# Neighbourhood attention in a two-layer backbone: two heads of a couple as one unit instead of one head after the other

## The chip, the cores and the metric

One Trainium2 chip, one of its cores. The metric is device time in microseconds (us) of one launch; lower is better. The kernel is written in Bass with the Tile framework: the program is Python that emits instructions, and a scheduler fixes, when the program is built, in which order each engine (TensorE = PE, VectorE = DVE, ScalarE = ACT, GpSimd = POOL, SyncE = SP) gets them. On the chip each engine takes its own list strictly in that order, and semaphores make it wait for the others.

## What is computed

Two trunk layers of a diffusion backbone over 384 tokens (128 context, 256 latent) of width 1024. In each layer the tokens go through an input projection, four mixing branches (retention, an S5 state-space scan, gated linear attention, neighbourhood attention), gates, a merge, an output projection and an MLP. The change is in the neighbourhood attention. It has 4 heads of 64 channels. For a block of 128 queries and a head, cut to what matters:

```python
s = q @ k.T * 0.125                 # context block: 128 keys; latent block: 256 latent keys + 128 cached context keys
s[:, :256] += bias                  # latent blocks only: a table with the window of neighbours
p = softmax(s)                      # over all keys of the row
o = p @ v
```

There are three blocks of queries (one context, two latent) and four heads, so 12 such pieces a layer.

## The kernel before, in words

Nearly all of TensorE's time is weights: a tile of 128 x 1024 float32 weights is loaded (`next_w`, L167), split into a rounded high part and a low part (ACT cast L143, DVE subtraction L155), and multiplied in three terms (L208, L209, L210), 24 matmuls a tile. Everything else is put between these: after each weight tile `step` (L193) advances every running background job, a Python generator, by its rate. In `mixers` (L1436) the jobs are the S5 scan (`s5_scan` L957, 31 dependent steps on POOL), `na_mix` (L1358, the neighbourhood attention, at `NA_RATE`), `gla_mix` and `ret_mix`. What the generators emit is then placed by the scheduler, so the order of an engine follows neither the text nor the generators alone.

`na_mix` takes one head at a time: for a pair `pr` of heads, a block `i` of queries and a head `par` of the pair it does

- scores on PE (L1377): q and k of head `par` lie in partitions 64*par to 64*par+63, so the matmul uses half of the array's rows and fills one PSUM bank (tag `my`, which `yps` gives out and of which there are only two); float32, so it goes through the array in two passes;
- for latent blocks a DMA of the bias table (L1380, SP queue), the sum on DVE (L1381) and a copy on ACT (L1382); for the context block a copy (L1384);
- softmax: maximum on DVE (L1386), exponential with its sum on ACT (L1387), reciprocal and scaling on DVE (L1388, L1389);
- then `yield`, and transposes on PE (L1393) into a second `my` bank, a copy on ACT (L1394), the values (L1397, half of the array's columns, one to three matmuls of two passes each), and a copy of 64 partitions into `q` (L1399).

Its scratch is the row buffer `rB`, three slots of 1024 columns in rotation. The whole job is 12 units of two yields, at rate 2: 12 weight tiles.

After the projection `mixers` waits for the S5 scan and the attention to be emitted (`finish`), then `s5_spread` (L985) takes `rB` over: two memsets on DVE (L990) and 12 copies on ACT (L994, L995, L996) of the scan's result. L994 and L996 read all time slots, so they need the last step of the scan; the S5 output matmuls (L1016, L1020) and the gates (`gates` L1405, their activation L1411 writes `rC`, which holds the scan's result) come behind. Beside them run the last parts of the gated linear attention (L1118, L1200 to L1232) and of the retention (L1287 to L1324).

Of the kernel before, what the change touches and what calls it, by code (L numbers as in the profile page):

```python
# [15 lines left out]
AF = mybir.ActivationFunctionType  # L16
ALU = mybir.AluOpType
ADD, SUB, MUL = ALU.add, ALU.subtract, ALU.mult
# [24 lines left out]
RAW4 = 4  # L43
LAG0 = 2
ADA_MIX, ADA_MLP, S5_MLP = (5, 4), (2, 1), (4, 1)
NA_RATE = 2
FOUR = ([((0, 1, 2), (k,)) for k in range(3)] + [((3,), range(3))] + [(range(4), (k,)) for k in range(3, 6)]
        + [((b,), (6, 7)) for b in range(4)])

# [5 lines left out]
class Kernel:  # L55
# [1302 lines left out]
    def na_mix(self, l):  # L1358
        nc = self.nc
        V, A = nc.vector, nc.scalar  # L1360
        q, k, v = self.nq, self.nk, self.nv
        cv = self.ft[:, 2694:2950]
        nc.gpsimd.dma_start(cv, self.d["na_v"][l])
        rb = self.row("rB", shape=(128, 3072))
        unit = 0
        for pr in range(2):
            for i in range(3):
                for par in range(2):

                    h = 2 * pr + par  # L1370
                    r = slice(64 * par, 64 * par + 64)
                    n = 384 if i else 128
                    o = 1024 * (unit % 3)
                    unit += 1
                    s, pT, bias = rb[:, o:o + n], rb[:, o + 384:o + 384 + n], rb[:, o + 768:o + 1024]
                    ps = self.yps()
                    nc.tensor.matmul(ps[:, 0:n], q[r, pr, 128 * i:128 * (i + 1)], k[r, pr, 128:512] if i else k[r, pr, 0:128],  # L1377
                                     start=True, stop=True)
                    if i:
                        nc.sync.dma_start(bias, self.d["na_bias"][l, pr, :, par, i - 1])  # L1380
                        V.tensor_tensor(s[:, 0:256], ps[:, 0:256], bias, op=ADD)  # L1381
                        A.copy(s[:, 256:384], ps[:, 256:384])  # L1382
                    else:
                        A.copy(s, ps[:, 0:n])  # L1384
                    mx, sm, rs = self.few(1), self.few(1), self.few(1)
                    V.tensor_reduce(mx, s, axis=mybir.AxisListType.X, op=ALU.max, negate=True)  # L1386
                    A.activation(s, s, AF.Exp, bias=mx, accum_out=sm)  # L1387
                    V.reciprocal(rs, sm)  # L1388
                    V.tensor_scalar(s, s, rs, None, op0=MUL)  # L1389
                    yield  # L1390
                    pt = self.yps()
                    for j in range(n // 128):
                        nc.tensor.transpose(pt[:, j * 128:(j + 1) * 128], s[:, j * 128:(j + 1) * 128], self.ident)  # L1393
                    A.copy(pT, pt[:, 0:n])  # L1394
                    vs = [v[:, 1], v[:, 2], cv] if i else [v[:, 0]]
                    for j, lv in enumerate(vs):
                        nc.tensor.matmul(pt[r, 384:512], lv[:, h * 64:(h + 1) * 64], pT[:, j * 128:(j + 1) * 128],  # L1397
                                         start=j == 0, stop=j == len(vs) - 1)
                    A.copy(q[r, pr, 128 * i:128 * (i + 1)], pt[r, 384:512])  # L1399
                    yield  # L1400
        self.out[3] = q


# [32 lines left out]
    def mixers(self, l, hs, hook, first):  # L1436
# [5 lines left out]
        self.na_in(l, hs, first)  # L1442
        na = self.start(self.na_mix(l), NA_RATE)
        self.gla_in(l, hs)
# [359 lines left out]
```

## Time and profile before

| | |
|---|---|
| runs, us | 1440.46, 1439.47, 1440.29 (median 1440.29) |
| the profiled execution, us | 1436.91 |
| its span from first to last instruction, us | 1435.0 |
| granted TensorE clock, mean | 0.993 |
| PE busy | 1383.7 us, 96% |
| DVE, ACT, POOL busy | 65%, 46%, 24% |

PE is the bound, so an instruction on another engine costs time only where PE comes to wait for it. A row of the timeline gives the start, the duration, the engine, the line, the operation and, in brackets, the idle time ahead of it with what ended it. Matmuls overlap in the array: what one costs is the distance from its start to the next start, not its duration.

### The profile page before, as it was taken

How to read it: one execution, taken by the hardware profiler on the slowest of the kernel's cores; microseconds unless marked ns; L12 is line 12 of the kernel's file. 1: busy time of each engine (PE TensorE's matmuls, PEld its weight loads, DVE VectorE, ACT ScalarE, POOL GpSimd, SP SyncE). 2: the span in 40 equal slices, each digit the busy share in tenths (PEclk: the TensorE clock that was granted, in tenths of full speed). 3: DMA queues.
4: the chain of work that ended last, by engine and by line, in shares of the span. 5: the costliest groups of instructions: out<-in, count | busy, mean ns of one | idle time of the engine just before them, and what ended most of it. 6: DMA issues, size and time to landing. Idle time of an engine off the chain costs nothing. (4 is left out here: it accounts for less than half of the span.)

```text
span 1435.0 us, 22364 instructions
## 1 busy us (share of the span) xinstructions
PE 1383.7 (96%) x8492; PEld 1230.5 (86%) x8492; DVE 936.5 (65%) x1480; ACT 664.1 (46%) x1235; POOL 350.5 (24%) x654
## 2 busy tenths in 40 slices
PE   6979999999999999999999999999999999999998
PEld 5857867899998888888988888698999789999896
DVE  4598972699875868777363388448995658333334
ACT  3446563433336544443464555643433465444433
POOL 5964691001121123320011592000011200000000
PEclk9999999999999999999999999999999999999999
DMA  9446433477553656666446433146764536333442
GB/s 383 150 132 188 148 103 82 158 231 238 191 177 131 196 181 202 197 216 205 151 144 198 144 102 105 56 140 211 250 218 133 205 104 220 132 125 125 136 150 82
DMA packets 93628, 238.17 MB, mean 166 GB/s; under 512 B 17968, under 2 KB 39504, under 8 KB 93520
## 3 DMA queue, kind: packets, MB, share of 16 engines
q1 hardware_dynamic: 90656, 227.75, 49.0%
q0 software_dynamic: 2864, 8.98, 1.9%
q8 instruction: 67, 1.10, 0.3%
q14 instruction: 41, 0.34, 0.1%
HBM read 221.72 MB, written 14.97 MB: 165 GB/s over the span
## 5 line engine op out<-in xcount | busy, mean ns | idle before, releaser
L155 DVE TENSOR_TENSOR wl<-wf,wh 128x1024 fp32r<-128x1024 f32 (+1 forms) x254 | 320.6, 1265 | 269.8 <-ACT wh L143 269.2
L143 ACT CAST wh<-wf 128x1024 fp32r<-128x1024 f32 (+1 forms) x254 | 264.4, 1045 | 433.5 <-PE mx L209 175.2
L208 PE MATMUL mm<-hh,wh 128*128 128x384 f32 (+1 forms) x712 | 243.8, 342 | 1.4 <-ACT fb L879 1.4
L210 PE MATMUL mm<-hh,wl 128*128 128x384 f32 (+1 forms) x712 | 242.6, 342 | 1.1 <-DVE wl L155 1.1
L209 PE MATMUL mm<-hl,wh 128*128 128x384 f32 (+1 forms) x712 | 242.3, 340 | 0.0
L208 PE MATMUL mx<-hh,wh 128*128 128x384 f32 x448 | 151.1, 337 | 0.0
L210 PE MATMUL mx<-hh,wl 128*128 128x384 f32 x448 | 150.5, 336 | 0.0
L209 PE MATMUL mx<-hl,wh 128*128 128x384 f32 x448 | 150.4, 336 | 0.0
L210 PEld LDWEIGHTS mm<-hh,wl 128*128 128x128 f32 (+1 forms) x712 | 133.0, 187 | 7.3 <-issue 4.0
L208 PEld LDWEIGHTS mm<-hh,wh 128*128 128x128 f32 (+1 forms) x712 | 133.0, 187 | 6.7 <-issue 2.8
L209 PEld LDWEIGHTS mm<-hl,wh 128*128 128x128 f32 (+1 forms) x712 | 133.1, 187 | 6.2 <-issue 4.2
L604 DVE SCALAR_TENSOR_TENSOR mid<-r,fa 128x1024 f32<-128x1024 f32 x80 | 102.6, 1283 | 30.9 <-DMA r<-w_ada 20.6
L604 DVE SCALAR_TENSOR_TENSOR mid<-r,fb 128x1024 f32<-128x1024 f32 x80 | 100.1, 1251 | 0.2
L209 PE MATMUL mm<-wl,rA 128*128 128x512 f32 x216 | 85.7, 397 | 1.5 <-DVE wl L155 1.5
L208 PEld LDWEIGHTS mx<-hh,wh 128*128 128x128 f32 x448 | 84.2, 188 | 2.8 <-issue 1.0
L209 PEld LDWEIGHTS mx<-hl,wh 128*128 128x128 f32 x448 | 84.2, 188 | 1.8
L210 PEld LDWEIGHTS mx<-hh,wl 128*128 128x128 f32 x448 | 84.2, 188 | 0.2
L208 PE MATMUL mm<-wh,rA 128*128 128x512 f32 x216 | 79.5, 397 | 0.7 <-ACT rA L121 0.7
L210 PE MATMUL mm<-wh,rB 128*128 128x512 f32 x180 | 70.2, 392 | 0.0
L1431 POOL TENSOR_TENSOR c<-c,c 128x384 f32<-128x384 f32 x16 | 16.6, 1038 | 189.8 <-DVE c L1429 115.6
L706 POOL TENSOR_TENSOR few<-few,negh 128x1 f32<-128x1 f32 x24 | 13.3, 555 | 200.7 <-DVE few L705 194.6
L121 ACT CAST rA<-c 128x384 fp32r<-128x384 f32 x80 | 41.1, 514 | 40.4 <-DVE c L1433 38.6
(539 smaller groups left out, 2940.9 us busy)
## 6 DMA issues: line engine op xcount, KB each, us to landing
wf<-w_mlp SPq DMA_DIRECT2D x128, 512.0 KB, 3.5
r<-w_ada SPq DMA_DIRECT2D x82, 512.0 KB, 4.2
wf<-w_merge SPq DMA_DIRECT2D x64, 512.0 KB, 4.0
wf<-w_in SPq DMA_DIRECT2D x43, 512.0 KB, 4.0
wf<-w_branch SPq DMA_DIRECT2D x16, 512.0 KB, 4.1
wf<-w_out SPq DMA_DIRECT2D x16, 512.0 KB, 3.5
s_vt<-mid SPq DMA_DIRECT2D x16, 256.0 KB, 3.1
mid<-s_vt SPq DMA_DIRECT2D x8, 512.0 KB, 5.0
```

The costliest lines, as they stand in the source:

```text
L121: self.nc.scalar.copy(hi, src)
L143: self.nc.scalar.copy(wh[:, :cols], raw)
L155: self.nc.vector.tensor_tensor(wl[:, :cols], raw, wh[:, :cols].bitcast(F32), op=SUB)
L208: mm(out, lh, rh, start=start, stop=False)
L209: mm(out, lh, rl, start=False, stop=False)
L210: mm(out, ll, rh, start=False, stop=stop)
L604: nc.vector.scalar_tensor_tensor(self.mid([128, D]), w, 0.5, self.cb[g], op0=MUL, op1=MUL, accum_out=mod[:, n, g:g + 1])
L706: self.nc.gpsimd.tensor_tensor(r, v, self.negh[:, 0:1], op=ALU.pow)
L1431: nc.gpsimd.tensor_tensor(us[0], us[0], us[1], op=ADD)
```

## The change

The head leaves the loop and becomes a loop inside the unit: both scores go into two banks, then the softmax of the one and of the other, then the transposes of both into two banks, then the values of both into two halves of the partitions of one bank, alternating between the heads, and one copy of 128 partitions into `q`. The bias tables move into four slots behind the two heads' scratch, which no longer rotates: every unit uses the same two slots. There are six units of two yields a layer, and `NA_RATE` is 1, so the job still takes 12 weight tiles.

```diff
--- before.py
+++ after.py
@@ -43,7 +43,7 @@
 RAW4 = 4
 LAG0 = 2
 ADA_MIX, ADA_MLP, S5_MLP = (5, 4), (2, 1), (4, 1)
-NA_RATE = 2
+NA_RATE = 1
 FOUR = ([((0, 1, 2), (k,)) for k in range(3)] + [((3,), range(3))] + [(range(4), (k,)) for k in range(3, 6)]
         + [((b,), (6, 7)) for b in range(4)])
 
@@ -1362,42 +1362,51 @@
         cv = self.ft[:, 2694:2950]
         nc.gpsimd.dma_start(cv, self.d["na_v"][l])
         rb = self.row("rB", shape=(128, 3072))
-        unit = 0
-        for pr in range(2):
-            for i in range(3):
+        for u in range(6):
+
+
+            pr, i = divmod(u, 3)
+            n = 384 if i else 128
+            qs = slice(128 * i, 128 * (i + 1))
+            w = [rb[:, o:o + 1024] for o in (0, 1024)]
+            s = [t[:, 0:n] for t in w]
+            ps = [self.yps() for _ in w]
+            for par in range(2):
+                r = slice(64 * par, 64 * par + 64)
+                nc.tensor.matmul(ps[par][:, 0:n], q[r, pr, qs], k[r, pr, 128:512] if i else k[r, pr, 0:128],
+                                 start=True, stop=True)
+            for par in range(2):
+                if i:
+                    bias = rb[:, 2048 + 256 * (2 * (u % 2) + par):][:, 0:256]
+                    nc.sync.dma_start(bias, self.d["na_bias"][l, pr, :, par, i - 1])
+                    V.tensor_tensor(s[par][:, 0:256], ps[par][:, 0:256], bias, op=ADD)
+                    A.copy(s[par][:, 256:384], ps[par][:, 256:384])
+                else:
+                    A.copy(s[par], ps[par][:, 0:n])
+            mx, sm, rs = self.few(2), self.few(2), self.few(2)
+            for par in range(2):
+                c = slice(par, par + 1)
+                V.tensor_reduce(mx[:, c], s[par], axis=mybir.AxisListType.X, op=ALU.max, negate=True)
+                A.activation(s[par], s[par], AF.Exp, bias=mx[:, c], accum_out=sm[:, c])
+            for par in range(2):
+                c = slice(par, par + 1)
+                V.reciprocal(rs[:, c], sm[:, c])
+                V.tensor_scalar(s[par], s[par], rs[:, c], None, op0=MUL)
+            yield
+            pt = [self.yps() for _ in w]
+            pT = [t[:, 384:384 + n] for t in w]
+            for par in range(2):
+                for j in range(n // 128):
+                    nc.tensor.transpose(pt[par][:, j * 128:(j + 1) * 128], s[par][:, j * 128:(j + 1) * 128], self.ident)
+                A.copy(pT[par], pt[par][:, 0:n])
+            vs = [v[:, 1], v[:, 2], cv] if i else [v[:, 0]]
+            for j, lv in enumerate(vs):
                 for par in range(2):
-
                     h = 2 * pr + par
-                    r = slice(64 * par, 64 * par + 64)
-                    n = 384 if i else 128
-                    o = 1024 * (unit % 3)
-                    unit += 1
-                    s, pT, bias = rb[:, o:o + n], rb[:, o + 384:o + 384 + n], rb[:, o + 768:o + 1024]
-                    ps = self.yps()
-                    nc.tensor.matmul(ps[:, 0:n], q[r, pr, 128 * i:128 * (i + 1)], k[r, pr, 128:512] if i else k[r, pr, 0:128],
-                                     start=True, stop=True)
-                    if i:
-                        nc.sync.dma_start(bias, self.d["na_bias"][l, pr, :, par, i - 1])
-                        V.tensor_tensor(s[:, 0:256], ps[:, 0:256], bias, op=ADD)
-                        A.copy(s[:, 256:384], ps[:, 256:384])
-                    else:
-                        A.copy(s, ps[:, 0:n])
-                    mx, sm, rs = self.few(1), self.few(1), self.few(1)
-                    V.tensor_reduce(mx, s, axis=mybir.AxisListType.X, op=ALU.max, negate=True)
-                    A.activation(s, s, AF.Exp, bias=mx, accum_out=sm)
-                    V.reciprocal(rs, sm)
-                    V.tensor_scalar(s, s, rs, None, op0=MUL)
-                    yield
-                    pt = self.yps()
-                    for j in range(n // 128):
-                        nc.tensor.transpose(pt[:, j * 128:(j + 1) * 128], s[:, j * 128:(j + 1) * 128], self.ident)
-                    A.copy(pT, pt[:, 0:n])
-                    vs = [v[:, 1], v[:, 2], cv] if i else [v[:, 0]]
-                    for j, lv in enumerate(vs):
-                        nc.tensor.matmul(pt[r, 384:512], lv[:, h * 64:(h + 1) * 64], pT[:, j * 128:(j + 1) * 128],
-                                         start=j == 0, stop=j == len(vs) - 1)
-                    A.copy(q[r, pr, 128 * i:128 * (i + 1)], pt[r, 384:512])
-                    yield
+                    nc.tensor.matmul(pt[0][64 * par:64 * par + 64, 384:512], lv[:, h * 64:(h + 1) * 64],
+                                     pT[par][:, j * 128:(j + 1) * 128], start=j == 0, stop=j == len(vs) - 1)
+            A.copy(q[:, pr, qs], pt[0][:, 384:512])
+            yield
         self.out[3] = q
 
 
```

What the scheduler makes of it, at three places. On PE around the third and fourth piece of layer 0, before (L1377 scores, L1393 transposes, L1397 values, `mm` a weight tile, L532 and L566 the S5 set-up):

```order
L1393 MATMUL my_1226<-ident_76,rB_1051 128x128 x2
L1377 MATMUL my_1321<-fa_781,fb_782 128x384
L208 MATMUL mm_1281<-wh_1173,hh_394 128x256
...
L209 MATMUL mm_1479<-hl_395,wh_1282 128x384
L1397 MATMUL my_1226<-rB_1051,fb_782 64x128 [waits Activation_49]
L1397 MATMUL my_1226<-rB_1051,fb_782 64x128
L1397 MATMUL my_1226<-rB_1051,rE_780 64x128 [waits DMASW2_49]
L210 MATMUL mm_1479<-hh_394,wl_1283 128x384
```

and now (L1406 values, L1376 scores):

```order
L1406 MATMUL my_1317<-rB_1051,fb_782 64x128 [waits Activation_49]
L208 MATMUL mm_1471<-hh_394,wh_1278 128x384
...
L1406 MATMUL my_1317<-rB_1051,fb_782 64x128 [waits Activation_49]
L1406 MATMUL my_1317<-rB_1051,fb_782 64x128 x2
L1406 MATMUL my_1317<-rB_1051,rE_780 64x128 [waits DMASW2_49]
L1406 MATMUL my_1317<-rB_1051,rE_780 64x128
L1376 MATMUL my_1411<-fa_781,fb_782 128x384 [waits PE_49]
```

The first head's first value matmul now stands by itself, the other five alternate between the heads, and the first score of the next unit stands right behind them; that unit's second score follows 27 rows later (it needs a bank).

On PE at the end of the input projection of layer 0, before (`mm_2887` is the last projected weight tile; the attention still has two pieces to go):

```order
L210 MATMUL mm_2887<-hh_394,wl_2596 128x384
L1393 MATMUL my_2230<-ident_76,rB_1051 128x128 [waits DVE_49,Activation_49]
L1393 MATMUL my_2230<-ident_76,rB_1051 128x128 x2
L1200 MATMUL mx_2624<-rX_1003,g_490_2605 128x512 [waits PE_49,Activation_49]
L1200 MATMUL mx_2631<-rX_1003,g_490_2605 128x512 [waits PE_49]
L1287 MATMUL mx_2644<-ident_76,r_497_2637 128x128 [waits PE_49]
L1377 MATMUL my_2306<-fa_781,fb_782 128x384 [waits Activation_49]
L1397 MATMUL my_2230<-rB_1051,fb_782 64x128 [waits Activation_49]
```

and now (`mm_2863` is that weight tile):

```order
L210 MATMUL mm_2863<-hh_394,wl_2572 128x384
L1406 MATMUL my_2286<-rB_1051,fb_782 64x128 [waits Activation_49]
L1406 MATMUL my_2286<-rB_1051,fb_782 64x128 x2
L1406 MATMUL my_2286<-rB_1051,rE_780 64x128 x2
...
L1298 MATMUL my_2757<-r_479_2613,rs_2610 128x256
L1200 MATMUL mx_2600<-rX_1003,g_472_2581 128x512 [waits PE_49,Activation_49]
L1200 MATMUL mx_2607<-rX_1003,g_472_2581 128x512 [waits PE_49]
L1287 MATMUL mx_2620<-ident_76,r_479_2613 128x128 [waits PE_49]
L1020 MATMUL my_2646<-rB_2554,mid_2647 128x96 [waits DMAHW1_49,DVE_49,Activation_49]
```

The attention ends with the weight tile, and the first S5 output matmul that reads the spread scan (L1020) has moved up: it stands ahead of the retention's and the linear attention's L1291, L1206, L1210 and L1222, which stood ahead of it.

On ACT at the same place, before (L1201 and L1289 evict L1200's and L1287's banks, L1212 and L1208 the linear attention's):

```order
L1201 COPY rA_1004<-mx_2624 128x512 [waits PE_49]
L1201 COPY rA_1004<-mx_2631 128x512 [waits PE_49]
L1289 COPY c_499_2646<-mx_2644 128x128 [waits PE_49]
...
L1212 COPY g_520_2747<-mx_2745 128x256 [waits DMASW0_49,PE_49]
L1399 COPY fb_782<-my_2318 64x128 [waits PE_49]
L994 COPY rB_2578<-rC_1658 64x384 [waits DVE_49,DMAHW4_49,Activation_49,Pool_49]
L995 COPY rB_2578<-rC_1658 64x8x16
```

and now (L1420 is the gates' activation):

```order
L1198 COPY rX_1003<-g_473_2582 32x128 x4
L994 COPY rB_2554<-rC_1642 64x384 [waits Pool_49]
L996 COPY rB_2554<-rC_1642 64x8x32
...
L996 COPY rB_2554<-rC_1642 64x8x32
L1201 COPY rA_1004<-mx_2600 128x512 [waits PE_49]
L1201 COPY rA_1004<-mx_2607 128x512 [waits PE_49]
L1289 COPY c_481_2622<-mx_2620 128x128 [waits PE_49]
L1420 ACTIVATE rC_2569<-mm_2570,bmh_742 128x384 [waits Activation_49]
```

The copies of the scan, which wait for POOL, stood behind L1201, L1289, L1294, L1208, L1212 and L1308; now they stand ahead of all of these, which are in the same queue.

## Rows read from the trace of the kernel before

**Rows 1.** The page, busy time of each engine.

```profile
PE 1383.7 (96%) x8492; PEld 1230.5 (86%) x8492; DVE 936.5 (65%) x1480; ACT 664.1 (46%) x1235; POOL 350.5 (24%) x654
```

**Rows 2.** Timeline of PE, a piece's transposes and the next piece's scores.

```profile
109.24 0.49 PE L1393 MATMUL my<-ident,rB 128*128 128x128 f32 x3
109.66 0.91 PE L1377 MATMUL my<-fa,fb 64*128 64x384 f32 x2
110.50 0.38 PE L208 MATMUL mm<-wh,hh 128*128 128x256 f32 x1
```

**Rows 3.** Timeline of PE, a piece's values between matmuls of a weight tile.

```profile
113.72 0.34 PE L208 MATMUL mm<-hh,wh 128*128 128x384 f32 x1
113.89 0.34 PE L209 MATMUL mm<-hl,wh 128*128 128x384 f32 x1
114.16 0.65 PE L1397 MATMUL my<-rB,fb 128*64 128x128 f32 x4
...
114.96 0.44 PE L210 MATMUL mm<-hh,wl 128*128 128x384 f32 x1
115.24 0.34 PE L208 MATMUL mm<-hh,wh 128*128 128x384 f32 x1
```

**Rows 4.** Timeline of PE in layer 1, scores with values right behind them.

```profile
905.19 0.91 PE L1377 MATMUL my<-fa,fb 64*128 64x384 f32 x2
906.03 0.65 PE L1397 MATMUL my<-rB,fb 128*64 128x128 f32 x4
...
906.83 0.49 PE L1291 MATMUL mx<-rD,c 128*128 128x128 f32 x2
```

**Rows 5.** Timeline of PE in layer 1, two heads' matmuls in the two column halves.

```profile
913.31 0.27 PE L1231 MATMUL mx<-rA,rE 128*64 128x128 f32 x1
913.37 0.27 PE L1229 MATMUL mx<-rA,rE 128*64 128x128 f32 x1
913.42 0.27 PE L1231 MATMUL mx<-rA,rE 128*64 128x128 f32 x1
```

**Rows 6.** Timeline of POOL, the scan of layer 0: first step, sixteenth, last instruction.

```profile
153.13 0.36 POOL L976 TENSOR_TENSOR sm<-sm,rC 128x64 f32<-128x64 f32 x1 [26.97 <-ACT rC L953]
...
195.93 0.61 POOL L979 TENSOR_TENSOR rC<-sm,sm 128x32 f32<-128x32 f32 x1
...
219.41 0.26 POOL L981 TENSOR_TENSOR rC<-sm,sm 128x32 f32<-128x32 f32 x1
```

**Rows 7.** Timeline of PE, layer 0, between the last projected and the next weight tile.

```profile
202.57 0.45 PE L210 MATMUL mm<-hh,wl 128*128 128x384 f32 x1
...
223.92 1.13 PE L1298 MATMUL my<-r,rs 128*128 128x256 f32 x4
...
226.08 0.35 PE L1020 MATMUL my<-rB,mid 128*128 128x96 f32 x1 [0.45 <-ACT rB L994]
...
235.27 0.63 PE L208 MATMUL mm<-hh,wh 128*128 128x384 f32 x1
```

**Rows 8.** Timeline of ACT, the first copy of the spread in layer 0.

```profile
222.66 0.51 ACT L994 COPY rB<-rC 64x384 f32<-64x384 f32 x1
```

**Rows 9.** Windows: us, busy us of PE, PEld, DVE, ACT, POOL, granted clock, DMA.

```profile
75.00:82.00 7.00, 0.19 (x2) 0.00 (x0) 7.00 (x8) 0.11 (x1) 5.12 (x8) 0.83 0.53 163
82.00:92.00 10.00, 9.95 (x51) 7.15 (x52) 10.00 (x27) 7.97 (x17) 0.99 (x1) 0.78 0.23 72
200.00:220.00 20.00, 15.37 (x83) 9.24 (x80) 6.91 (x17) 12.10 (x37) 17.71 (x68) 0.91 0.26 79
220.00:240.00 20.00, 19.44 (x122) 15.17 (x119) 6.17 (x11) 9.34 (x25) 1.04 (x2) 1.00 0.34 93
900.00:920.00 20.00, 17.94 (x110) 12.78 (x109) 7.92 (x20) 11.82 (x36) 1.08 (x2) 1.00 0.26 90
920.00:940.00 20.00, 18.78 (x109) 15.07 (x109) 6.60 (x12) 9.45 (x25) 1.89 (x1) 0.91 0.21 49
210.39:219.10 8.71, 5.81 (x38) 4.10 (x38) 4.05 (x11) 3.97 (x15) 7.88 (x30) 1.00 0.31 90
```

## The prediction

> **What bounds the kernel now.** First the busy times of the page: TensorE (PE) is busy 1383.7 of 1435.0 us [rows 1], so a saving counts where PE has no idle time, and a new cost counts where PE comes to wait. Then the timeline of PE around the pieces of attention, for the price of one block of scores and one of values; then the windows, for the stretches in which PE idles or its clock is low; then POOL's and ACT's timeline there, for what ends the wait. All sums are made against the profiled execution, 1436.9 us, whose span is 1435.0; the median of the runs is 1440.3, so 3.4 is added at the end. About 0.2% (2.9 us) is what a measurement of this kernel can tell from no change.
>
> **What a block costs on PE.** A weight matmul follows its predecessor by 0.17 us [rows 3]. The score block of 384 keys takes 0.84 us from its first start to the next matmul, and the three transposes ahead of it take 0.42 where three of 0.107 would take 0.32, so 0.10 goes on entering [rows 2]. A block of values takes 0.80 from start to start, the distances ahead of it and behind it are 0.27 and 0.28 instead of 0.17 [rows 3]: about 1.0 us, of which six passes of 0.109 are 0.65. So a block has 0.35 to 0.40 us in which the array computes nothing: I take 0.38 for entering and leaving half of the array. Where values follow scores at once, the two blocks take 0.84 and 0.80 and one crossing of 0.2 is shared [rows 4]: I take 0.22 saved for each such neighbour. Where two heads of the linear attention use the two column halves (L1229 and L1231, one bank), their passes start 0.05 us apart instead of 0.11 [rows 5]: the halves work at the same time.
>
> **What the change takes from PE.** The order of the instructions gives the counts. Values: a latent unit had two blocks of six passes, 12 x 0.109 = 1.31; now mostly one matmul alone (two passes, 0.22) and five alternating (ten passes at 0.054, 0.54), so 0.55 less; there are eight latent units, of which one has all six side by side (0.65 less), and in two of the four context units the values stand side by side (0.22 each): 2.4 us in layer 0 and 2.5 in layer 1. Blocks: 24 a layer before; now 22 in layer 0 and 21 in layer 1, 0.38 each: 0.8 and 1.1. Neighbours: one a layer before, five now, 4 x 0.22 = 0.9 each. Together **4.1 us in layer 0 and 4.5 in layer 1**. What is not gained: the pair of scores stands side by side only in the first unit of a layer, because the second score of each later unit waits for a bank. The Trainium skill's "TensorEngine Tiling (Array Packing)", Restrictions and Gotchas, says that row tiles write to different PSUM banks and so raise the pressure on PSUM; that speaks against this pairing, and the order agrees: with two banks, ten of twelve pairs are split. Had they stood together, ten more blocks of 0.38 would go, 3.8 us off the sum, which goes by the split order.
>
> **What it leaves alone.** ACT has 12 copies fewer (the two of 64 partitions become one), off the path. The 16 bias DMAs on SP's queue are the same number, and the weight loads there are moved past none that they wait for; I cost this at nothing, since DVE, which needs the bias, is busy 65% [rows 1]; if a bias came late, DVE's sum would hold the weight split queued behind it. The slots no longer rotate, so a unit's copies of scores wait for the former unit's values; the values now come right ahead of the scores, so nothing new is late. The first wait of layer 0 (PE does 0.19 us in 75 to 82 [rows 9]) stays: DVE's list there has the same operations in the same order, with one maximum more.
>
> **Layer 0's end: a loss.** The S5 scan on POOL runs from 153.13 to 219.67 [rows 6]. The last projected weight tile ends at 202.8, the next one starts at 235.27 [rows 7]; between them PE idles 4.6 + 0.6 us and has a clock of 0.91 in the first window [rows 9]. Before, ACT evicted the retention's and the linear attention's banks while the scan ran, so that PE did their matmuls: in 210.39 to 219.10 it was busy 5.8 of 8.7 us [rows 9], of which I count 0.9 for the attention's transposes and L1016, so 4.9 us of theirs. Now the copy L994, which needs the last step of the scan, stands ahead of these evictions on ACT, and L1020, which needs L994, ahead of these matmuls on PE. PE has done all that it may by about 208 and waits for POOL. After the scan's end S it then has: 2.9 us until L1020 can run through (from the first L994 at 222.66 to the last wait that ended at 226.08 it is 3.4 [rows 7, 8], with four copies of L995 less in between), the 15.6 us that it had between S and the next weight tile, less 0.6 idle, 0.2 of attention and 1.1 for L1298, which now comes earlier [rows 7, 9], and the 4.9 that were done before S: 21.5 against 15.6, **+5.9**. The long wait lowers the clock: after the wait of 75 to 82 the next 10 us ran at 0.78, which is 2.2 us lost [rows 9]; **+2.2** here (bounds 0 and 3.5, if the wait of some 14 us costs more than that one of 7). And S itself: the scan waits for ACT's copies (26.97 us of idle, L953 [rows 6]) of the last matmul of L947. Ahead of that matmul now stand 16 more weight matmuls (16 x 0.17 = 2.8), three more score blocks, two transposes and two values (3.5 by the prices above), less some 3.0 of what the change saves till there: 3.3 later. Against it, POOL's steps are slow while DVE splits weights (16 steps in 43.4 us, then 15 in 22.6 [rows 6]), and this splitting ends earlier beside the scan: I take **+1.5**, between -2 and +3.3. Layer 0: 5.9 + 2.2 + 1.5 = **+9.6**; of its own 4.1 us of savings 3.0 are in the start of the scan, and the rest is lost in the wait.
>
> **Layer 1's end: a gain.** There the scan ends long before, and the attention was late: PE idles 2.1 + 1.2 us in 900 to 940 and has a clock of 0.91 in the second half, 1.8 us [rows 9]. Now the attention ends with the weights and weight tiles come between the small matmuls. L1020 still waits for memsets and copies once, some 1.5 us, and I leave 1 us for other waits: 0.8 of idle less, and the 1.8 of the clock. With 4.5: **-7.1** (bounds -9.6, if all idle time goes, and -2.0, if the values don't overlap and no wait goes).
>
> **The sum.** +9.6 - 7.1 = +2.5: 1439.4 for the profiled execution, and **1443 us** for the median (1436.9 + 2.5 + 3.4 = 1442.8), a loss near the bound of what can be told.
>
> **Rivals.** (a) *Faster*: the scan doesn't hold the end of layer 0. For it: POOL's steps take half as long beside a quiet DVE, and DVE is quiet earlier; against it: the scan's first step comes later. The place is the copy L994 on ACT; the sign turns where layer 0 loses less than 7.1, that is with S at 218.7 or earlier instead of 221.2. With S 2 us ahead of before, no cold clock and layer 1 at its best: 5.9 - 2 - 9.6 = -5.7, so 1434.6; about 1434. (b) *Clearly slower*: the same place, with S 3.3 us later, a cold clock of 3.5, and in layer 1 PE's waits kept, so that only the 4.5 is gained there: 5.9 + 3.3 + 3.5 - 4.5 = +8.2, so 1448.5. For it: PE would wait 15 us and more, twice the wait of 75 to 82. (c) *The change doesn't do what it says*: alternating values of two heads go through the array in turn. Against it: [rows 5], where another two heads' do not; for it: nothing but that no row shows L1397's own heads at once. Layer 1 then gains 2.5 less and the scan starts some 1.3 later: +2.5 + 3.8 = +6.3, so 1446.6.
>
> **How the numbers follow.** The forecast gets 0.43 and lies between 1440 and 1446: half of it, 0.21, is over 1443.2 (slower), 0.20 within 0.2%, 0.02 faster. (a) gets 0.29, nearly all faster (0.28, and 0.01 the same). (b) gets 0.20, slower. (c) gets 0.08, slower but for 0.01. Faster 0.30, same 0.22, slower 0.48. The range takes in (a) and (b) near their middles: 1433 to 1450. The forecast's own range is 1440 to 1446.
>
> **What would show it.** In the profile after: L1406 passes 0.05 us apart; L994 of layer 0 at the end of POOL's scan near 221 with ACT idle ahead of it; PE idle over 10 us just ahead of L1020 in layer 0, and a clock below 0.9 behind it; the next weight tile near 230, but 14 matmuls later the small ones that stood ahead; in layer 1 weights between them and hardly any idle time in PE. It is wrong if PE doesn't wait for the scan in layer 0, if the scan starts earlier than 153, or if layer 1 keeps its idle time.

## The result and the profile after

The changed kernel takes **1460.97 us** (median of 4 runs, 1459.03 to 1463.20) against 1440.38 for the kernel before beside it (4 runs): a ratio of 1.0133, 95% interval 1.0099 to 1.0166. It is slower, as forecast, but by 20.6 us where 2.5 were forecast, and outside the range. The profiled execution has a span of 1461.0 us (before 1435.0), its mean granted clock is 0.979 (before 0.993).

The page's busy times, to be laid beside [rows 1]:

```profile
span 1461.0 us, 22351 instructions
PE 1394.3 (95%) x8492; PEld 1239.7 (85%) x8492; DVE 933.3 (64%) x1480; ACT 661.5 (45%) x1223; POOL 353.4 (24%) x654
```

PE's idle time is the span less its busy time: 66.7 us, before 51.3, so 15.4 more. Its busy time also grew, by 10.6, though it has the same 8492 matmuls. The windows say why. First before, then after; the columns are the stretch, its length, PE's busy us with the count of its instructions, the granted clock, the DMA engines' busy share and GB/s. A granted clock of 1.00 is TensorE's full level (2.4 GHz), 0.50 the half one (1.2 GHz); a value between is a mean of both over the stretch.

```profile
105.00:130.00 25.00, 22.51 (x142) 1.00 0.46 136
200.00:220.00 20.00, 15.37 (x83) 0.91 0.26 79
220.00:240.00 20.00, 19.44 (x122) 1.00 0.34 93
240.00:300.00 60.00, 60.00 (x353) 1.00 0.50 157
300.00:400.00 100.00, 98.54 (x581) 1.00 0.67 216
900.00:940.00 40.00, 36.73 (x218) 0.96 0.23 69
1000.00:1100.00 100.00, 100.00 (x593) 1.00 0.64 211
```

```profile
105.00:130.00 25.00, 24.75 (x107) 0.67 0.41 129
200.00:220.00 20.00, 14.79 (x94) 0.91 0.24 81
220.00:240.00 20.00, 8.66 (x40) 0.52 0.13 32
240.00:300.00 60.00, 60.00 (x369) 0.96 0.34 107
300.00:400.00 100.00, 94.58 (x522) 0.98 0.66 220
900.00:940.00 40.00, 38.32 (x269) 1.00 0.33 110
1000.00:1100.00 100.00, 95.34 (x527) 0.98 0.66 218
```

What the clock takes in a stretch is the busy time by one less the clock. Three places lose: 105 to 130 (24.75 x 0.33 = 8.2 us of clock, against 2.2 us less of idle), 200 to 300 (11.4 us more idle, 6.5 more of clock), and the two merges, 300 to 400 and 1000 to 1100 (4.0 and 4.7 us more idle, 1.9 of clock each). The end of layer 1's mixers, 900 to 940, gains: 1.6 idle and 1.5 clock. Summed over the whole span in stretches of 5 us, low clock takes 22.1 us after and 6.7 before, so 15.4 more. What is left, **busy time at full clock**, is 1394.3 - 22.1 = 1372.2 after and 1383.7 - 6.7 = 1377.0 before: 4.8 us less. So the 26.0 us are +15.4 idle, +15.4 low clock and -4.8 of work. The change does what it says on PE, and loses six times as much beside it. This account is of one execution each: the medians differ by 20.6 us and not by 26.0. The profiled execution of the kernel before (1436.9 us, granted clock 0.993) is a favourable one: the 47 runs of that kernel beside the experiments have medians of 1441.4 us and 0.987. So a part of the 15.4 us of low clock belongs to that execution and not to the change.

At the end of layer 0 the forecast mechanism stands in the timelines of POOL, ACT and PE (the scan's last instruction, the spread's first copy, the first matmul that needs it, the next weight tile); the first and the last answer to [rows 6, 7], the second to [rows 8]:

```profile
228.95 0.26 POOL L981 TENSOR_TENSOR rC<-sm,sm 128x32 f32<-128x32 f32 x1
...
229.24 0.51 ACT L994 COPY rB<-rC 64x384 f32<-64x384 f32 x1 [14.94 <-POOL rC L981]
...
231.34 2.31 PE L1020 MATMUL my<-rB,mid 128*128 128x96 f32 x8 [13.46 <-ACT rB L994]
...
241.69 0.67 PE L208 MATMUL mm<-hh,wh 128*128 128x384 f32 x1
```

ACT stands idle for 14.94 us in front of a copy that needs the scan, with the evictions behind it; PE for 13.46. But the scan ends at 229.21, not at 221.2, and begins at 164.01 (before 153.13). PE's longest waits in 60 to 130 before, then after, and after's in 300 to 420 (what waits, for what, us in total, times, longest):

```profile
PE my L1393 <- DVE rB L1389: 8.5, 2, 6.9
PE mx L532 <- DVE c L573: 1.5, 1, 1.5
PE mm L208 <- ACT fb L879: 1.4, 1, 1.4
...
PE mx L532 <- DVE c L573: 4.2, 1, 4.2
PE mm L210 <- DVE wl L155: 2.4, 1, 2.4
PE mm L208 <- ACT fb L879: 2.3, 1, 2.3
...
PE mm L208 <- ACT rC L1420: 3.1, 1, 3.1
PE my L209 <- DVE rX L122: 1.0, 1, 1.0
PE mx L208 <- ACT wh L143: 1.0, 1, 1.0
```

The wait of 6.9 us at 75 [rows 9] that was to stay is gone; two waits that stood there before are longer (1.5 to 4.2 us and 1.4 to 2.3), one of 2.4 is new, and the half clock of 105 to 122 follows the one of 4.2. In sum PE idles 2.1 us less in 60 to 130. At the merge, where it waited 1.4 us before, PE waits for the gates (L1420, before L1411): the retention's norm comes out later than the weights that need it. Its L902 on DVE runs at 332.39, before at 301.70.

### The profile page after: what moved, and what is told of

Its sections match the earlier page's. It is cut to its first block, busy times and chain, and to the rows that moved or that the text cites. A ratio compares the mean times of both kernels' runs of the same rounds, so it can differ in the third digit from the quotient of the medians.

```text
span 1461.0 us, 22351 instructions
## 1 busy us (share of the span) xinstructions
PE 1394.3 (95%) x8492; PEld 1239.7 (85%) x8492; DVE 933.3 (64%) x1480; ACT 661.5 (45%) x1223; POOL 353.4 (24%) x654
## 5 line engine op out<-in xcount | busy, mean ns | idle before, releaser
L210 PE MATMUL mm<-hh,wl 128*128 128x384 f32 (+1 forms) x712 | 245.6, 345 | 2.4 <-DVE wl L155 2.4
L706 POOL TENSOR_TENSOR few<-few,negh 128x1 f32<-128x1 f32 x24 | 13.3, 555 | 201.5 <-DVE few L705 195.2
L1440 POOL TENSOR_TENSOR c<-c,c 128x384 f32<-128x384 f32 x16 | 17.6, 1100 | 181.9 <-DVE c L1438 117.6
```

The source lines that it names most:

```text
L210: mm(out, ll, rh, start=False, stop=stop)
L706: self.nc.gpsimd.tensor_tensor(r, v, self.negh[:, 0:1], op=ALU.pow)
L1440: nc.gpsimd.tensor_tensor(us[0], us[0], us[1], op=ADD)
```

## The experiments

All profiles in one table. S is the end of layer 0's scan, the next column the start of the 49th of 240 weight tiles (behind layer 0's merge), then the time from there to the 173rd (behind layer 1's merge); idle, clock and work are as above. The ratio is to the runs of the kernel before that were made beside each experiment (medians 1440.4 to 1441.8; the row of before has the last 20). From S on the columns are of one profiled execution, which isn't always a typical one: those of a_late (1451.2 us), a_late_dma (1447.3) and a_both_dma2 (1447.6) are the lowest of their runs, that of a_both_dma (1454.1) is the highest. Experiments on the changed kernel begin with a, those on the kernel before with b.

| | median us (runs) | ratio, 95% | S | tile 49 | to tile 173 | span | idle | clock | work |
|---|---|---|---|---|---|---|---|---|---|
| before | 1441.8 (20) | 1 | 219.7 | 361.8 | 713.1 | 1435.0 | 51.3 | 6.7 | 1377.0 |
| after | 1461.0 (4) | 1.0099 to 1.0166 | 229.2 | 387.7 | 712.6 | 1461.0 | 66.7 | 22.1 | 1372.2 |
| a_rep | 1465.2 (1) | | 225.4 | 383.4 | 719.3 | 1462.8 | 66.5 | 25.5 | 1370.8 |
| a_seqval | 1474.0 (2) | 1.0135 to 1.0292 | 227.1 | 386.6 | 731.7 | 1478.6 | 69.1 | 35.4 | 1374.1 |
| a_rate2 | 1460.7 (2) | 1.0061 to 1.0181 | 224.0 | 382.1 | 714.2 | 1456.4 | 65.5 | 20.7 | 1370.2 |
| a_dma | 1463.7 (5) | 1.0118 to 1.0190 | 217.8 | 377.3 | 723.6 | 1461.8 | 66.3 | 25.7 | 1369.8 |
| a_late | 1458.7 (4) | 1.0062 to 1.0183 | 224.1 | 374.4 | 714.7 | 1449.1 | 60.7 | 15.7 | 1372.7 |
| a_late_dma | 1455.1 (5) | 1.0062 to 1.0140 | 216.1 | 366.4 | 714.5 | 1445.3 | 56.4 | 17.6 | 1371.3 |
| a_both_dma | 1450.5 (7) | 1.0038 to 1.0083 | 219.3 | 370.4 | 720.0 | 1452.2 | 52.7 | 27.3 | 1372.2 |
| a_both_dma2 | 1451.6 (9) | 1.0046 to 1.0092 | 220.7 | 367.1 | 718.0 | 1445.7 | 53.4 | 20.5 | 1371.8 |
| b_swap | 1455.6 (5) | 1.0057 to 1.0116 | 224.6 | 381.6 | 712.1 | 1453.7 | 62.0 | 15.9 | 1375.8 |
| b_dma | 1446.2 (10) | 0.9988 to 1.0053 | 221.8 | 371.5 | 713.9 | 1446.1 | 49.9 | 18.1 | 1378.1 |
| b_late_dma | 1452.9 (6) | 1.0040 to 1.0091 | 221.3 | 370.8 | 719.0 | 1451.7 | 53.0 | 20.1 | 1378.6 |
| b_both_dma | 1450.3 (12) | 1.0029 to 1.0082 | 224.3 | 374.1 | 712.8 | 1450.1 | 53.9 | 20.3 | 1375.9 |

**Is it the pairing? The order of the two heads alone (b_swap).**

```diff
-                for par in range(2):
+                for par in (1, 0):
```

> The kernel before, one head at a time, but the second head of each couple first: the same instructions, the same sizes, another order of the heads. The scheduler then puts the first L994 of layer 0 ahead of L1294, L1208 and L1212 on ACT, and L1020 ahead of L1206, L1210 and L1222 on PE, much as in the changed kernel. Theory (the place of the spread costs the time): 4 to 10 us slower than before, 1444 to 1450, with a wait of L1020 for L994 of 4 us or more in layer 0. Rival (the pairing of the heads costs the time): within 3 us of before, since nothing is paired here.

The kernel before with the odd head ahead of the even one: the same instructions and nearly the same work (1375.8, before 1377.0), and 14 us slower, more than the 4 to 10 expected. PE's waits in 200 to 260 and the longest in 300 to 420:

```profile
PE my L1020 <- ACT rB L994: 12.6, 2, 12.4
...
PE mm L208 <- ACT rC L1411: 3.0, 1, 3.0
```

These are the changed kernel's waits of layer 0, without any pairing (at layer 1's merge PE waits for nothing here). They belong to an order of the engines that the scheduler also reaches from the kernel before.

**Do the two heads' values overlap? One head's after the other's (a_seqval).**

```diff
-            for j, lv in enumerate(vs):
-                for par in range(2):
-                    h = 2 * pr + par
+            for par in range(2):
+                h = 2 * pr + par
+                for j, lv in enumerate(vs):
```

> The changed kernel with the values head by head (all matmuls of the one head, then all of the other) instead of alternating. Theory of my prediction (alternating halves the time of the values, 2.4 us a layer): where PE is the bound the time of the values rises from 0.054 to 0.109 us a pass, 2 to 5 us slower in all than the changed kernel. Rival (PE lets a matmul of the free column half start anyway): the passes still start 0.054 us apart and nothing is lost. In both cases the spread of layer 0 stands even further ahead on ACT (ahead of L1170, L1198 and L1201), so the wait in layer 0 should be some 3 to 6 us longer than in the changed kernel: 1463 to 1470.

PE's timeline around one unit's values, first after, then this kernel:

```profile
149.56 0.32 PE L1406 MATMUL my<-rB,fb 128*64 128x128 f32 x1
...
149.70 0.51 PE L1406 MATMUL my<-rB,fb 128*64 128x128 f32 x5
149.94 0.49 PE L1406 MATMUL my<-rB,rE 128*64 128x128 f32 x4
150.36 0.48 PE L1376 MATMUL my<-fa,fb 64*128 64x128 f32 x2
```

```profile
148.29 0.65 PE L1406 MATMUL my<-rB,fb 128*64 128x128 f32 x4
148.78 0.38 PE L1406 MATMUL my<-rB,rE 128*64 128x128 f32 x2
149.09 0.48 PE L1376 MATMUL my<-fa,fb 64*128 64x128 f32 x2
```

From the first value to the next score both take 0.80 us, with ten passes of two heads alternating and with the six of one head. Summed over layer 1, the distances behind value matmuls are 5.39 us after, 7.11 here and 7.81 before. The overlap is there. The time of this kernel, 13 us over the changed one (two runs, 1467.5 and 1480.5; 1463 to 1470 was expected), is not its price: in the profiled execution, 17.6 us longer, the work is only 1.9 us more, and the rest is 2.4 us more idle and 13.3 more low clock. About 10 of the 13.3 stand in a stretch of 20 us from 500 on, with no wait of 1 us ahead of it.

**The pace of the attention (a_rate2).**

```diff
-NA_RATE = 1
+NA_RATE = 2
```

> The changed kernel with the rate of the attention's job at 2 as before, so that its six units are emitted within 6 weight tiles instead of 12. Theory (the place of the spread in layer 0 costs the time): L994 stands at the same place in ACT's list as in the changed kernel, so the time is within 5 of 1461. Rival (the lower rate makes the attention end late and holds rB): 10 us or more faster than the changed kernel.

Nothing changes that can be told, as expected by the theory: 1460.65, PE still waits 11.9 us for L994. How fast the job is emitted is not the point.

**The spread behind the evictions, in layer 0 (a_late).** Two pieces of the linear attention and one of the retention are emitted ahead of the spread, and its ACT copies are ordered behind theirs.

```diff
         self.finish(s5, na)
+        ret = self.start(self.ret_mix(l))
+        act = self.nc.scalar.engine
+        if l == 0:
+            last = []
+            for j in list(self.jobs):
+                if j[0] in (gla, ret):
+                    for _ in range(2 if j[0] is gla else 1):
+                        self.piece(j)
+                    last.append([i.name for i in self.traced() if i.engine == act][-1 if j[0] is ret else -3])
+        n = len(self.traced())
         self.s5_spread()
-        ret = self.start(self.ret_mix(l))
+        if l == 0:
+            for i in self.traced()[n:]:
+                if i.engine == act:
+                    for name in last:
+                        self.no_sync(i, name)
```

> The changed kernel, but in layer 0 the remaining pieces of the linear attention and the first piece of the retention are emitted ahead of the spread of the scan, and ACT's copies of the spread are ordered behind their evictions (L1212, L1232, L1294): on ACT L994 now follows all of these, as before the change. Theory (the scan holds the end of layer 0 because the spread stands ahead of the evictions): the 13.5 us wait of L1020 falls below 4, the low clock behind it goes, and 9 to 13 of the 26 us come back, about 1450. Rival (two heads in one unit cost the time themselves, on PE, DVE or in the clock before 150 us): the time stays within 4 of 1461, the idle time only moves to another line of the same stretch. The low clock between 105 and 122 us stays by both.

The wait for L994 falls from 13.5 to 2.8 us, and tile 49 starts 13.3 us earlier than after (374.4). But the work that was let through meets the next wait: a load on POOL's queue, issued only when the scan has left POOL. PE's main waits in 200 to 260, and then the longest at layer 1's merge, where the spread stands where it stood (in 300 to 420 PE waits for nothing):

```profile
PE mx L1222 <- DMA g<-st_gla: 7.3, 1, 7.3
...
PE my L1020 <- ACT rB L994: 2.8, 2, 2.3
...
PE mm L208 <- ACT rC L1420: 3.0, 1, 3.0
```

The merge's waits went in the layer in which the spread was moved, and stayed in the other. The time is inconclusive: four runs, two at 1451 to 1453 and two at 1464 to 1465; the profile is of the lowest, and the median is only 2.2 us under the changed kernel.

**With the loads off POOL's queue (a_late_dma, b_dma, b_late_dma).** Beside the edit above, three loads of states go to SP's queue.

```diff
-        P.dma_start(s0, self.d["st_gla"][l])
+        nc.sync.dma_start(s0, self.d["st_gla"][l])
...
-        nc.gpsimd.dma_start(s0, self.d["st_ret"][l])
+        nc.sync.dma_start(s0, self.d["st_ret"][l])
-        nc.gpsimd.dma_start(u, self.d["c_up"])
+        nc.sync.dma_start(u, self.d["c_up"])
```

> The kernel of the run a_late (changed kernel, in layer 0 the spread of the scan behind the evictions of the linear attention and the retention), and the three small loads of their states (L1193, L1270, L1272) go through SP's queue instead of POOL's, where they stood behind the scan. Theory (layer 0 is held by what is queued behind POOL's scan): the wait of 7.3 us of L1222 for st_gla goes, PE then waits only for the scan itself, which ends at 224 to 229; some 4 us faster than a_late, 1448 to 1455. Rival (the scan's own end holds everything, whatever stands ahead of it): L1020's wait grows by what L1222's loses, and the time is that of a_late within 2.

> The kernel before with only the three small loads moved from POOL's queue to SP's. Theory (what is queued behind the scan costs the end of layer 0): the waits of L1222 (1.2 us) and around it go, 0 to 3 us faster than before. Rival (every change of the emitted program shifts the engines' order, and the kernel before is a lucky draw among such orders): 5 to 15 us slower, though no operation is added.

> The kernel before with the same two edits as a_late_dma (spread of layer 0 behind the evictions, loads on SP's queue), so that it differs from a_late_dma by the pairing of the heads alone. Theory (pairing is worth some us where PE is the bound, and its loss came from the place of the spread): this one is within 3 us of before, and a_late_dma is within 5 us of it, on either side. Rival (pairing itself costs 10 us or more, in the stretch up to 150 us by DVE's longer units and the low clock): a_late_dma is 8 to 15 us slower than this one.

The wait of 7.3 us is gone, and with the pairing the time is 1455.1, 3.6 under a_late; the scan ended at 216.1, though, and not at 224 to 229. In the kernel before the loads alone change nothing that can be told (the interval holds 1), and both edits make it slower by 0.4 to 0.9%, where within 3 us was expected. Paired and unpaired with the same two edits stand at 1455.1 and 1452.9, within the 5 us expected, with intervals that overlap.

**Both layers (a_both_dma, b_both_dma, a_both_dma2).** The edits of a_late without the condition on the layer, and the loads; b_both_dma is the kernel before with the same.

```diff
-        if l == 0:
+        if True:
```

> As a_late_dma, with the spread behind the evictions in layer 1 too, and so the retention's and the linear attention's chain earlier there. Theory (the 7 us that layer 1 gained were given back at its merge, because weights were drawn ahead of the retention's chain and the head norms then stood bare): the waits at the merge of layer 1 (L1420 3.0, L143 1.0, and others, 5 to 6 us) go, and it is 4 to 6 us faster than a_late_dma. Rival (the merge waits come from something else, as weights or the gates' buffers): they stay within 1 us.

> The kernel before with the loads on SP's queue and the copies of the spread behind the evictions in both layers, so that it differs from the changed kernel with the same two edits by the pairing alone. Theory (the pairing itself is worth about nothing, since what it takes from PE is less than what single orders scatter by): the two are within 4 us of each other, this one at 1446 to 1454. Rival, that the pairing's own 4 to 5 us a layer come through once the order is alike: this one is 6 to 9 us slower than its counterpart. Rival, that the pairing costs: it is over 4 us faster.

> The changed kernel with both edits in both layers once more, on the same chip and beside the same runs of the kernel before as its counterpart without pairing. Theory: 1449 to 1453, as the first time (1450.5), and within 4 us of the counterpart.

PE's waits of a_both_dma in 200 to 260 and then at both merges, all that there are above 0.5 us:

```profile
PE my L1020 <- ACT rB L994: 2.5, 2, 2.3
PE mx L1200 <- ACT rX L1198: 2.5, 1, 2.5
PE mx L1291 <- ACT c L1289: 1.2, 2, 0.7
...
PE mm L208 <- DVE c L1438: 0.6, 1, 0.6
...
PE mm L208 <- DVE c L1438: 0.6, 1, 0.6
```

The merge's waits are now gone in layer 1 too. 1450.5 and 1451.6 are the best times with the pairing, about 10 us under the changed kernel and 9 to 10 over the kernel before, and a_both_dma is the expected 4 to 6 us under a_late_dma (4.6). The profiles don't show a gain in layer 1, though (718 to 720 us to tile 173, 714.5 in a_late_dma): low clock behind other waits, 7 to 10 us in 900 to 1000, took more than the merge gave; with one execution of each this is not a measure of the edit. b_both_dma, which differs by the pairing alone, stands at 1450.3. So at a like order **the pairing is worth nothing that can be told**: the rival by which its own 4 to 5 us a layer come through (6 to 9 us) is not borne out, nor is one by which it costs. The work is some 4 us less with the pairing (1372.2 and 1371.8 against 1375.9), but its runs show a lower granted clock: 0.979 and 0.978 on the mean of 7 and 9 runs against 0.982 of 12, which by estimate is 5 us of 1450 and about as much as the work saved. Why it is lower is not shown. No version here beats the kernel before.

**Two separate losses? The loads alone, and the changed kernel once more (a_dma, a_rep).**

> The changed kernel with only the three state loads (L1193, L1270, L1272) on SP's queue; the copies of the spread stay where the change has them. Moving the loads also moves instructions from the start of the program on, on DVE among others: the S5 set-up comes ahead of the weight splits that it followed in the changed kernel. Theory of two separate losses (an early one from DVE's order ahead of the scan, a late one from the copies of the spread ahead of the evictions): the wait of L532 for L573 at 105 us (4.2 us) and the half clock behind it are gone, the scan ends near 216 to 220 instead of 229, as in the version with both edits; the wait of L1020 for L994 of 11 to 15 us in layer 0 and the waits for L1420 at both merges stay. Time 1450 to 1457, against 1461 for the changed kernel and 1455 for both edits. Rival, that all of the loss hangs on the late placement: the scan end makes no difference and the time stays at 1459 to 1463. Second rival, that the early stage varies by itself from run to run: the scan ends at 225 or later here.

> The changed kernel unaltered, profiled once more. If the half clock of 105 to 122 us belongs to the order (a wait of 4.2 us of PE at 101 to 105), the wait shows again with the same length and the scan again starts near 164; if the length of the low clock is an accident of the execution, the wait shows again, the low clock is shorter (some 8 to 10 us, as in the two variants with the same wait), the scan starts at 158 to 160 and the span is 3 to 5 us shorter than 1461.0.

a_dma was expected at 1450 to 1457 and took 1463.7, a miss, nearer to the rival's 1459 to 1463. In layer 0 the theory held: the wait of 4.2 us and the half clock behind it are gone, S comes at 217.8, tile 49 starts 10.4 us earlier than after, and the wait for L994 (9.2) and those at the merge stay. The wait of 7.1 us at 75 to 82 stands there again, as in before. But from tile 49 to tile 173 it takes 723.6 us where after takes 712.6. The windows of a_dma in three of the stretches above, then of a_rep in two:

```profile
105.00:130.00 25.00, 23.03 (x141) 0.96 0.51 159
900.00:940.00 40.00, 38.26 (x230) 0.87 0.38 112
1000.00:1100.00 100.00, 91.82 (x505) 0.95 0.66 212
```

```profile
105.00:130.00 25.00, 25.00 (x130) 0.81 0.42 128
900.00:940.00 40.00, 38.32 (x250) 0.92 0.39 113
```

In a_dma layer 1's merge costs 8.2 us of idle time and 900 to 940 runs at a lower clock. a_rep is the changed kernel itself. Its waits are the same to a tenth (4.2, 2.5 and 2.2 in 60 to 130; 1.7 for L994 in layer 1), but the clock is not: 0.81 for 0.67 in 105 to 130, so that its scan starts 3.6 us earlier, and 0.92 for 1.00 in 900 to 940. What layer 0 gained, 4.3 us to tile 49, layer 1 lost (6.7), and the span is 1.8 us longer, where the second reading promised 3 to 5 less. The order of the instructions sets the waits; how long the clock stays low behind one differs between these two executions of one program.

## Why the prediction was wrong

**PE's savings: right in layer 1, over the whole program too large.** In layer 1 scores, transposes and values take 16.39 us from start to start, before 19.84, and 12 entries into half of the array are gone (16 blocks for 28), at the forecast's 0.10 each 1.2 more: about 4.6, forecast 4.5. In layer 0 the same distances hold idle time and low clock that have other causes, so they don't give the saving. The column "work" shows the whole: 1369.8 to 1372.7 us in the eight profiles with the two heads' values alternating, 1375.8 to 1378.6 in the five without pairing. On the mean that is 5.7 us (1371.4 and 1377.1), less than the 8.6 that was forecast for both layers. Rival (c), values that don't overlap, is out by a_seqval.

**The place of the loss: right.** L994 ahead of the evictions, L1020 ahead of the matmuls, ACT and PE idle until the scan ends: 13.46 us of PE, forecast over 10; the rival of 1434 us with it falls, since S came 9.5 us later, not earlier. Moving the copies (a_late) takes all but 2.8 us of the wait away.

**The sizes: wrong, in three steps.** First, "S itself: +1.5", and with it the clock ahead of the scan, at which the sum put nothing. S came 9.5 us later: the scan began 10.9 us later and was 1.3 us shorter. Of this, 8.2 us are the clock lost in 105 to 130. Less that, S is 1.3 us later; in a_rep, where the same stretch lost 4.7, S came 5.7 later, 1.0 less that. So the +1.5 was near, by these two executions, and what failed is that low clock was priced behind the wait for L994 alone. I had written that the first wait of layer 0 "stays", since DVE's list there has the same operations. That list doesn't decide it. On DVE, before, after and in a_dma, and PE's wait in a_dma:

```profile
73.99 6.41 DVE L395 TENSOR_TENSOR c<-mid,s5coef 128x256 f32<-128x256 f32 x1
```

```profile
75.38 0.42 DVE L395 TENSOR_TENSOR c<-mid,s5coef 128x256 f32<-128x256 f32 x1 [0.19 <-POOL s5coef L467]
```

```profile
73.92 6.37 DVE L395 TENSOR_TENSOR c<-mid,s5coef 128x256 f32<-128x256 f32 x1 [3.04 <-POOL s5coef L467]
...
PE my L1400 <- DVE rB L1394: 7.1, 1, 7.1
```

The same addition of the S5 set-up lasted 6.41 us before, and the softmax stood behind it; after it came 1.4 us later and lasted 0.42, though it started beside the same DMA issue of POOL (L1356) with the same POOL work behind it. So the wait of 75 went, and others came or grew: a weight split was late (2.4), then, with the second head's softmax and bias sum in DVE's list ahead of it, the set-up's L573, for which PE waits 4.2 us at 101 to 105. In a_dma and the other three paired profiles with the loads moved the addition is long again, the wait of 75 stays as forecast, and S is 216.1 to 220.7. So the pairing doesn't bring the early loss by itself; nor is it needed for it: in b_both_dma PE waits 3.2 us for L573, and S is 224.3. The low clock went with the wait (in a_dma both are gone), but a_dma's order differs in more than this; why L573 is late is read from the list alone. The prediction also laid sixteen steps of POOL in 43.4 us beside fifteen in 22.6, as the price of a busy DVE, and rival (a) leaned on it. The two are not alike: the early steps work on 128x64 and the late ones on 128x32 [rows 6].

Second, the cold clock, "+2.2, bounds 0 and 3.5". The 13.5 us wait and what follows it cost 6.5 us of clock more than before in 200 to 300. I had priced it by a wait of half the length [rows 9]. Here PE was busy from 231.34 on without a pause, with small matmuls, and the clock was still 0.52 in 220 to 240 and 0.96 in 240 to 300; why it stayed low for so long is not shown.

Third, **the merges were not in the sum at all**: 4.0 and 4.7 us of idle time and 1.9 of clock each, 12.5 together. I followed the evictions behind L994 to PE's next weight tile and stopped. They also feed the linear attention's and the retention's norms, whose results the merge's gates need over 100 us later. What was held back at 215 came due at 350, where PE stands and waits for it. That these waits hang on the place of the spread is shown by a_late and a_both_dma, where they go in the layers in which it was moved. In layer 1 PE did get its -7.1: 1.6 us of idle time and 1.5 of clock less in 900 to 940 and 4.6 of work; and the merge took 6.6 back, so that the layer is even (712.6 and 713.1 to tile 173).

So rival (b) named the right place with too small a price: 1448.5. Its "3.3 later" and "cold clock of 3.5" were the ends of my range for terms that came out at 9.5 and 6.5.

What stays open: why the kernel before stays 9 to 14 us under its own variants with another order (b_swap, b_late_dma, b_both_dma), which do nearly the same work, is not pinned to one instruction. Its profile has the least clock loss (6.7 us, the others 15.7 and more) and nearly the least idle time, but the clock loss is that of its favourable execution. Open is also how much of the 20.6 us each of the three steps costs on the median, since each was read from one or two executions.

## What to carry to other kernels

Follow every instruction that a late copy holds back to its last consumer, also when that is 100 us further on, and ask what cover is left there. When an edit lets a scheduler reorder a tuned kernel, the order can cost or give more than the edit: try a null edit (here the two heads swapped, +14 us) before crediting a change with its time. And keep the accounts in three columns, idle time, low clock and work at full clock; the last shows what the edit does on PE itself, and the other two scatter with the order and from run to run.

## What the runs showed of the hardware

Two row halves of the array work at once: the first pair of scores, two heads with two passes each, takes hardly longer than the two passes of one head (above, at 150.36, 0.48 us):

```profile
66.81 0.49 PE L1376 MATMUL my<-fa,fb 64*128 64x128 f32 x4
```

The addition on DVE shown above (L395) lasted 0.42 us in eight of the fourteen profiles, 2.46 in b_swap and 6.37 to 6.41 in the other five. Before, it stands from 73.99 to 80.40, while POOL ran eight instructions of 0.66 to 0.81 us end to end from 74.56 to 80.11; the first and the last of them:

```profile
74.56 0.81 POOL L398 TENSOR_TENSOR r<-r,g 128x288 f32<-128x288 f32 x1
...
79.45 0.66 POOL L397 TENSOR_TENSOR g<-mid,s5pw 128x288 f32<-128x288 f32 x1
```

The Trainium skill's "SBUF — State Buffer", section "SBUF: two separate sides", says that GpSimd and a DVE operation with two inputs from SBUF share a pair of ports, and that the one that comes second is blocked for the whole instruction of the other. The trace agrees in that the addition ends just behind POOL's run; but here it lasted through eight instructions of POOL and not one, and by the start times the addition came first, by 0.57 us. After, where it starts as shortly ahead of the same POOL instruction (75.38 and 75.95), it took 0.42. What decides between the two is not shown.

The granted clock behind the same wait of the same program was 0.67 over 25 us in one execution and 0.81 in another, and behind one of 1.7 us 1.00 and 0.92. The Trainium skill's "TensorE: Matmul & The Clock Gate", Part 1, says that the number of slow matmuls differs from run to run of one kernel, and tells it of a kernel's start; these traces show it in the middle of one. Single runs scatter with the clock: the 20 runs of the kernel before beside the last experiments lie between 1436.4 us (granted clock 0.991) and 1449.7 (0.983), so that one profile can't judge a change of a few us.
